# An encoder layer on one core: the gated unit's input split where it is made, reordered on another queue, and its first products in the last attention step

## The chip, the core and the metric

The kernel runs on one core of one Trainium2 chip. A core has a matrix engine (TensorE, PE in the profile, with its weight loads listed as PEld), a vector engine (DVE), a scalar engine (ACT), a general engine (GpSimd, POOL) and a synchronization engine (SyncE, SP). Data reach the on-chip memory SBUF through DMA transfers, which an engine's instruction queue issues; here SP, ACT and POOL all issue some. Each engine takes its instructions in order, so an instruction that waits holds back all that stand behind it on that engine, DMA issues included. Matrix products go into PSUM banks and are read from there by DVE or ACT.

The metric is the time of one execution in microseconds, less being better. The time before is the median of three runs, 1557.84 us (1557.83 to 1558.92).

## The reference

One encoder layer with shared weights is applied to two sequences of 512 tokens with 1024 features, in fp32. Cut to what matters:

```python
h = rms_norm(x, ln1)
q, k, v, u, g_att, g_ssm = split(h @ w_in)
y_att = windowed_attention(rms_norm(q), rms_norm(k), v, sink, bias, mask)   # 16 heads, 4 key/value heads, blocks of 128
y = gelu(s5(u, forward) + s5(u, backward) + d_skip * u)                     # state-space branch, 64 groups of 16 channels
y_ssm = y * sigmoid(y @ w_glu + b_glu)                                      # the gated unit
mixed = sigmoid(g_att) * y_att + sigmoid(g_ssm) * y_ssm
x = x + mixed @ w_out
out = x + square(relu(rms_norm(x, ln2) @ w_up)) @ w_down
```

The change concerns `y`, the output of the state-space branch, and the product `y @ w_glu` that reads it.

## The kernel before

**Products.** An fp32 product is made of three matmuls on rounded operands. An operand is split into a high part, its value rounded to fp32r by a copy on ACT, and a low part, the remainder, by a subtraction on DVE. `mm3` (L148 to L152) issues high times high, high times low, low times high into one PSUM bank. Products of the first half of the kernel share three banks, `acc()`; the `sps` banks are two.

**Stages.** In the trace of before: input norm and tables up to about 230 us; the scan of the state-space branch, a chain of DVE operations, 233 to 343 (L577 to L586); the state outputs, 343 to 430 (L599 to L630); the attention's prelude and steps, 430 to 734; the gated unit (L1030 to L1053), 711 to 833; the output product, the second norm and the MLP to the end. The MLP is a Strassen-like scheme and is not touched.

**State outputs.** The 64 groups are taken two at a time, in 32 rounds `q`. A round makes six matmuls of 128 columns into one `sps` bank (L612, L615), and Gelu (L619) writes the result into `ysb`. After every eight groups one DMA on ACT's queue (L629) stores `ysb` to `y_scr` in DRAM. Loads of the next `u_sb`, `toep` (every eight groups) and `ctab` (every four) stand on POOL's queue, one batch ahead. `pull` puts products of other input blocks between the rounds, and these fill PE.

**Attention.** There are four key/value heads `j` and two sequences `sq`, so eight steps; each has four query blocks `qb`, called units here. The order on PE, ACT and DVE is written out by hand in a manual schedule. Next to a unit's scores and softmax stand matmuls of the previous unit's values (`prev`) and, through `project`, 24 products of the next step's queries (`Tile.project`, L712). The last step has no next step, so its `project` is `nop`. `rows` is the Tile whose queries are turned next; `lower` is a weight split's second half, held until a later place. In a step's second and fourth unit `Divide` handles the previous step: it stores reciprocal row sums to `rs_scr` (L824) and loads them spread over partitions as `fac` (L829), both on SP's queue, and `multiply` (L834) applies them and stores to `mix_scr` (L835). Only the last Divide, after the steps, uses POOL's queue. The weights of the next heads are loaded on SP (L669) and split.

**Reorder of y.** `y_scr` has the chunk position `t` (eight of them) outermost, and the gated unit wants channels on partitions. Eight DMAs from DRAM to DRAM (L900, 512 KB each, on SP) in the units of steps 1 and 2 copy `y_scr[t]` into `y2_scr`.

**Tail and gated unit.** After step 6 the pool `hpool`, with the split input rows `hT`, is closed, and two slots `slot_a` and `slot_b` take its place, which hold the operands `yT`. After the last step the last unit's values are finished, the last Divide runs, and a loop over eight row blocks `m` loads y (L1007) and splits it for each sequence (L1012 on ACT, L1013 on DVE); the read of y has a step, which also puts the tokens into their order. Then the gated unit: for each weight column `m` the column is loaded and split (`c_hi` at L121, `c_lo` at L122), and for each sequence `s` three tiles are loaded on POOL's queue (L1037: attention output, and two gates), the sum of y's two parts gives y again (`yy`, L1043), two multiplications prepare the gates (L1044, L1045), 24 matmuls make the product (`proj_T`), ACT applies the sigmoid (L1048), DVE multiplies and adds (L1049, L1050), and the result is split into `mixT` (L1051, L1052). After each column one row of `w_out` is loaded and split (L1024 to L1026). The second half of `w_out` goes into `slot_a` once the gated unit has read it. `out_half` then makes the output product of each block of 128 tokens and half of `w_out`, 24 matmuls each.

Of the kernel before, what the change touches and what calls it, by code (L numbers as in the profile page):

```python
# [12 lines left out]
F32 = mybir.dt.float32  # L13
# [6 lines left out]
P = 128  # L20
# [20 lines left out]
CH = 16  # L41
# [22 lines left out]
def hybrid_layer(ctx, tc, x, rel, onehot, ln1, w_qkv, w_ug, vectors, lam, coefs, w_glu, w_out, ln2,  # L64
# [15 lines left out]
    def acc():  # L80
        return ps_acc.tile([P, 512], F32, tag="acc", name="acc")
# [8 lines left out]
    y_scr = dram.tile([T, CH, GROUPS, NSEQ * NCHUNK], F32, name="y_scr")  # L90
    y2_scr = dram.tile([GROUPS, CH, T, NSEQ * NCHUNK], F32, name="y2_scr")
# [62 lines left out]
    def proj_T(w, m, act):  # L154

        ps = acc()
        for k in range(KT):
            ws = [t[:, k, m * P:(m + 1) * P] for t in w]
            mm3(ps, ws, [t[:, k, :] for t in act], k == 0, k == KT - 1)
        return ps  # L160
# [5 lines left out]
    hpool_cm = tc.tile_pool(name="hpool", bufs=1, side="right")  # L166
    hpool = hpool_cm.__enter__()
    hT = [[hpool.tile([P, KT, HALF], F32R, name=f"hT{s}_{i}") for i in range(2)] for s in range(NSEQ)]
# [261 lines left out]
    with tc.tile_pool(name="hst", bufs=1) as hp:  # L430
# [127 lines left out]
        with tc.tile_pool(name="ssmo", bufs=2) as sp:  # L558
# [20 lines left out]
            for i in range(1, NCHUNK - 1):  # L579
                t1 = sp.tile([P, 2, GROUPS, NSEQ], F32, tag="t1", name="t1", bufs=1)  # L580
                t2 = sp.tile([P, 2, GROUPS, NSEQ], F32, tag="t2", name="t2", bufs=1)
                V.tensor_mul(t1, h[:, i], a8r)
                V.tensor_mul(t2, h[:, i, ::-1], a8i)
                V.tensor_add(t1, t1, h[:, i + 1])
                V.tensor_add(h[:, i + 1], t1, t2)
                pull(15)  # L586
# [12 lines left out]

            states = [state_rows(0), state_rows(1)]  # L600
            for q in range(GROUPS // SH):
                g0 = q * SH
                if g0 % SB == 0:
                    u_sb, toep = ahead.pop(0)
                    ysb = sp.tile([P, SB, NSEQ * NCHUNK], F32, tag="ysb", name="ysb")
                if g0 % SI == 0:
                    ctab = ahead_c.pop(0)
                st = states.pop(0)
                ps = sps()
                for g in range(SH):  # L610
                    o = ps[:, g * P:(g + 1) * P]
                    PE.matmul(o, toep[:, g0 % SB + g].rearrange("p t c -> p (t c)"), u_sb[:, g0 % SB + g, :],  # L612
                              start=True, stop=False)
                    for ri in range(2):
                        PE.matmul(o, ctab[:, g0 % SI + g, ri, 0:T * CH],  # L615
                                  st[:, ri, g].rearrange("p s k -> p (s k)"), start=False, stop=ri == 1)
                if q + 2 < GROUPS // SH:
                    states.append(state_rows(q + 2))
                S.activation(ysb[:, g0 % SB:g0 % SB + SH, :].rearrange("p g k -> p (g k)"), ps[:, 0:SH * P],  # L619
                             AF.Gelu_apprx_tanh)  # L620

                pull(-(-(phase["units"] - 84) // (GROUPS // SH - q)))
                if (g0 + SH) % SI == 0 and g0 + SH + 2 * SI < GROUPS:
                    ahead_c.append(load_table(g0 + SH + 2 * SI))
                if (g0 + SH) % SB == 0 and g0 + SH + SB < GROUPS:
                    ahead.append(load_batch(g0 + SH + SB))
                if (g0 + SH) % SB == 0:
                    ga = g0 + SH - SB
                    S.dma_start(y_scr[:, :, ga:ga + SB].rearrange("t c g k -> (t c) (g k)"),  # L629
                                ysb.rearrange("p g k -> p (g k)"))  # L630
# [4 lines left out]
    with tc.tile_pool(name="att", bufs=2, reuse_waits="tile") as ap, tc.tile_pool(name="attc", bufs=1, reuse_waits="tile") as ac:  # L635
# [63 lines left out]
        class Tile:  # L699


            def __init__(self, j, sq, t):
                self.key, self.t, self.k, self.qn = (j, sq), t, 0, None
                self.ps = acc()[:, 0:CB]
# [26 lines left out]
            def turn(self):  # L731
                self.pt = acc()
                for h in range(G):
                    PE.transpose(self.pt[0:64, h * P:(h + 1) * P], self.qn[:, h], ident)
# [102 lines left out]

        def whole_block(src, pool, tag, bufs):
# [37 lines left out]
        def nop(*_):  # L876
            pass

        def pieces_of(i):

            if i == 0:
                return weight_pieces(1)
            if i % 2 == 1:
                pending[:] = weight_pieces(i // 2 + 2) if i // 2 + 2 < N_KV else []
                return pending[:2]
            return pending[2:]

        pending = []
        prev = owed = lower = None
        with tc.manual_schedule(engines={mybir.EngineType.PE, mybir.EngineType.Activation, mybir.EngineType.DVE}):  # L890
            for i, (j, sq) in enumerate(steps):
# [4 lines left out]
                for qb in range(NB):  # L896
                    if 1 <= i < 3:

                        t = (i - 1) * NB + qb
                        SP.dma_start(y2_scr[:, :, t, :].rearrange("g c k -> c g k"), y_scr[t])  # L900
# [4 lines left out]
                    project = new.project if new else nop  # L905
                    kd = None
                    if rows and not rows.qn:
                        rows.power()
# [78 lines left out]
                if i == len(steps) - 2:  # L987
                    hpool_cm.__exit__(None, None, None)
                    slot_a = opers.enter_context(tc.tile_pool(name="slot_a", bufs=1, side="right", reuse_waits="tile"))
                    slot_b = opers.enter_context(tc.tile_pool(name="slot_b", bufs=1, side="right", reuse_waits="tile"))  # L990
                    yT = [slot(slot_b), slot(slot_a)]
        owed.add()
        for k in range(prev.nkb):
            prev.turn(k)
            prev.high(k)
            prev.low(k)
            prev.value(k, 0)
            prev.value(k, 1)
        prev.lower_part()
        prev.add()  # L1000
        div = Divide(*steps[-1], *done, True)
        div.invert()
        div.turn()
        div.multiply()
        for m in range(KT):
            yr = (ap if m % 2 else evp).tile([P, T, NSEQ, NCHUNK], F32, tag="c_lo" if m % 2 else "ev", name="yr")
            SP.dma_start(yr.rearrange("p t s k -> p (t s k)"),  # L1007
                         y2_scr[m * 8:(m + 1) * 8].rearrange("g c t k -> (g c) (t k)"))
            for sy in range(NSEQ):
                yv = yr[:, :, sy, :].rearrange("p t k -> p k t")  # L1010
                hi = yT[sy][0][:, m, :].rearrange("p (k t) -> p k t", t=T)
                S.copy(hi, yv)  # L1012
                V.tensor_sub(yT[sy][1][:, m, :].rearrange("p (k t) -> p k t", t=T), yv, hi.bitcast(F32))  # L1013

# [15 lines left out]
    with tc.tile_pool(name="glu", bufs=3, reuse_waits="tile") as gpool:  # L1030
        for m in range(KT):
            w = load_column(w_glu[m], V.tensor_sub)
            for s in range(NSEQ):
# [9 lines left out]
                V.tensor_add(yy, yT[s][0][:, m, :].bitcast(F32), yT[s][1][:, m, :].bitcast(F32))  # L1043
                V.tensor_mul(gs_, gs_, yy)  # L1044
                V.tensor_mul(at, at, ga)  # L1045
                ps = proj_T(w, 0, yT[s])
                gl = gpool.tile([P, HALF], F32, tag="gl", name="gl", bufs=2)
                S.activation(gl, ps, AF.Sigmoid, bias=bglu_sb[:, m:m + 1])  # L1048
# [349 lines left out]
```

## Time and profile before

| | us |
|---|---|
| median of three runs | 1557.84 |
| the profiled execution | 1555.4 |
| its span in the profile | 1553.6 |
| state outputs | about 343 to 430 |
| attention steps 0 to 7, by their row-sum multiplications (L834) of the first and the last | 531.8 to 732.4 |
| products of the gated unit | 711.5 to 826.0 |
| its elementwise work | 741.2 to 833.4 |

The profile is of one execution, so its span is set against that execution's own time: 1.8 us lie around the span. The mean granted clock of TensorE was 0.985 of full speed. DMA moved 237 MB, 165.35 MB read from HBM and 81.82 MB written.

How to read the views: a row of the page's groups names the line, the engine, the operation, its output and inputs with partitions x elements, the count, then busy time and the mean of one instruction in ns, then the idle time of the engine just before and what ended it. A row of the view of stretches gives start and end, length, then busy time with counts for PE, PEld, DVE, ACT and POOL, the granted clock, the DMA share and the rate in GB/s. A row of the timeline gives the start, the duration, engine and line, and in brackets what the instruction waited for. An engine with the letter q (SPq, ACTq) is its queue of DMA issues.

### The profile page before, as it was taken

The numbers are of one execution on the slowest core, as the hardware profiler recorded it, in microseconds if no ns is written. First come the engines' busy times: TensorE is split into PE (matmuls) and PEld (weight loads), VectorE is DVE, ScalarE is ACT, GpSimd is POOL, SyncE is SP. The second block draws the span as 40 slices with busy tenths as digits, with TensorE's granted clock in tenths as the row PEclk, the third lists the DMA queues.
The fourth block names the chain that finished last, engine by engine and source line by source line (L and its number), as shares of the span: only waits on it lengthen the run. The fifth ranks groups of instructions, "written<-read, shape, count | busy, mean of one in ns | idle before, by whom it ended". The sixth has DMA issues, their size and how long they took to land.

```text
span 1553.6 us, 21555 instructions
## 1 busy us (share of the span) xinstructions
PE 1474.7 (95%) x7818; PEld 1246.7 (80%) x7818; DVE 1110.6 (71%) x1997; ACT 768.1 (49%) x1349; POOL 200.6 (13%) x372
## 2 busy tenths in 40 slices
PE   5799999999999899988699989999999999999998
PEld 4688888888999898976577877888888888888787
DVE  8679849994436789887866548777777578666553
ACT  6577761234436687786333325545445434433332
POOL 3033332002331222211320000000000000000000
PEclk9899999999999999999899999999999999999999
DMA  5644448227751413214755214444444595455342
GB/s 181 213 139 164 144 155 297 102 95 272 265 170 40 110 47 84 85 55 141 255 158 166 95 71 160 149 149 150 149 155 150 194 359 198 149 163 163 122 123 67
DMA packets 103531, 237.07 MB, mean 153 GB/s; under 512 B 11994, under 2 KB 31706, under 8 KB 103424
## 3 DMA queue, kind: packets, MB, share of 16 engines
q1 hardware_dynamic: 64784, 134.82, 27.3%
q0 software_dynamic: 16464, 50.39, 9.8%
q10 hardware_dynamic: 22176, 50.47, 8.5%
q8 instruction: 62, 1.02, 0.3%
q14 instruction: 45, 0.37, 0.1%
HBM read 165.35 MB, written 81.82 MB: 159 GB/s over the span
## 4 chain that ended last, share of the span: by engine, by line
PE 53%; issue 17%; DVE 6%; DMA 3%; ACT 3%; POOL 3%; POOLq 0%; SPq 0%; DVEq 0%; ACTq 0%
PE bank L151 13%; PE bank L152 13%; PE bank L150 13%; PE acc L712 3%; PE po L795 2%; PE acc L261 1%; PE sps L763 1%; POOL mx L1037 1%; DVE pl L788 1%; PE tps L779 1%; PE sps L615 1%; DVE p L767 1%; PE acc L150 1%; PE acc L151 1%; PE acc L152 1%
## 5 line engine op out<-in xcount | busy, mean ns | idle before, releaser
L221 PE MATMUL acc<-hT,c_hi 128*128 128x512 f32 x768 | 249.9, 401 | 0.8 <-ACT c_hi L211 0.8
L151 PE MATMUL bank<-b_lo,a_hi 128*128 128x512 f32 x448 | 174.7, 390 | 1.2 <-DVE b_lo L1267 1.2
L152 PE MATMUL bank<-b_hi,a_lo 128*128 128x512 f32 x448 | 174.6, 390 | 0.0
L150 PE MATMUL bank<-b_hi,a_hi 128*128 128x512 f32 x448 | 173.7, 390 | 0.0
L221 PEld LDWEIGHTS acc<-hT,c_hi 128*128 128x128 f32 x768 | 142.5, 190 | 29.9 <-issue 2.2
L221 PE MATMUL acc<-hT,c_lo 128*128 128x512 f32 x384 | 153.3, 400 | 0.5 <-DVE c_lo L212 0.5
L150 PE MATMUL bank<-act,act 128*128 128x512 f32 x376 | 147.3, 392 | 2.2 <-ACT act L1162 2.2
L1266 ACT CAST a_hi<-d_a 128x1024 fp32r<-128x1024 f32 x56 | 58.9, 1052 | 179.1 <-PE bank L151 177.5
L151 PE MATMUL bank<-act,act 128*128 128x512 f32 x376 | 147.1, 391 | 0.0
L152 PE MATMUL bank<-act,act 128*128 128x512 f32 x376 | 146.9, 391 | 0.0
L1267 DVE TENSOR_TENSOR a_lo<-d_a,a_hi 128x1024 fp32r<-128x1024 f32 x56 | 68.5, 1224 | 100.2 <-ACT a_hi L1266 100.2
L712 PE MATMUL acc<-w_hi,hT 128*128 128x256 f32 x512 | 116.1, 295 | 0.0
L151 PEld LDWEIGHTS bank<-b_lo,a_hi 128*128 128x128 f32 x448 | 84.2, 188 | 19.4 <-DVE b_lo L1267 1.9
L152 PEld LDWEIGHTS bank<-b_hi,a_lo 128*128 128x128 f32 x448 | 84.1, 188 | 17.3
L150 PEld LDWEIGHTS bank<-b_hi,a_hi 128*128 128x128 f32 x448 | 84.1, 188 | 17.3
L712 PEld LDWEIGHTS acc<-w_hi,hT 128*128 128x128 f32 x512 | 87.0, 189 | 3.7
L221 PEld LDWEIGHTS acc<-hT,c_lo 128*128 128x128 f32 x384 | 72.9, 190 | 15.2 <-issue 1.0
L773 ACT ACTIVATE p<-p,nmx 128x257 f32<-128x257 f32 (+1 forms) x128 | 72.2, 564 | 25.7 <-DVE nmx L767 24.6
L150 PEld LDWEIGHTS bank<-act,act 128*128 128x128 f32 x376 | 71.0, 189 | 17.4 <-ACT act L1162 2.7
L152 PEld LDWEIGHTS bank<-act,act 128*128 128x128 f32 x376 | 71.0, 189 | 14.9
L151 PEld LDWEIGHTS bank<-act,act 128*128 128x128 f32 x376 | 71.1, 189 | 14.6
L767 DVE CUSTOM_DVE_ANT_0 p<-sps,bias,vec 128x256 f32<-128x256 f32 (+1 forms) x128 | 69.1, 541 | 6.8 <-PE sps L763 5.6
(315 smaller groups left out, 3495.0 us busy)
## 6 DMA issues: line engine op xcount, KB each, us to landing
d_a<-a_scr SPq DMA_DIRECT2D x56, 512.0 KB, 3.6
u_raw<-in_w_up_dram SPq DMA_DIRECT2D x32, 512.0 KB, 5.6
a_scr<-t ACTq DMA_DIRECT2D x64, 256.0 KB, 5.1
k<-in_w_down_dram SPq DMA_DIRECT2D x32, 512.0 KB, 6.0
c_raw<-in_w_ug_dram SPq DMA_DIRECT2D x48, 256.0 KB, 3.3
a_scr<-a ACTq DMA_DIRECT2D x48, 256.0 KB, 2.1
ct_scr<-ctab POOLq DMA_DIRECT2D x16, 576.0 KB, 4.5
ctab_in<-ct_scr POOLq DMA_DIRECT2D x16, 576.0 KB, 7.3
```

Of the source, the lines that this page charges most:

```text
L150: PE.matmul(ps, a[0], b[0], start=first, stop=False)
L151: PE.matmul(ps, a[0], b[1], start=False, stop=False)
L152: PE.matmul(ps, a[1], b[0], start=False, stop=last)
L221: PE.matmul(ps, w[wi][:, k, :], hT[s][hi][:, k, :], start=n == 0, stop=n == 3 * KT - 1)
L261: PE.matmul(ps, hT[t // 4][act][:, k, (t % 4) * P:(t % 4 + 1) * P], wt[:, k % 4, :], start=n == 0, stop=n == 3 * KT - 1)
L615: PE.matmul(o, ctab[:, g0 % SI + g, ri, 0:T * CH], st[:, ri, g].rearrange("p s k -> p (s k)"), start=False, stop=ri == 1)
L712: PE.matmul(self.ps, hT[sq][act][:, k, col:col + P], w[:, k % 4, :], start=i == 0, stop=i == 3 * KT - 1)
L767: V.tensor_tensor_reduce(self.p[:, h, 1:1 + self.nk], self.s[h][:, 0:self.nk], biases[self.j][h][:, b0:b0 + self.nk], -1.0, nsink[:, hh:hh ...
L773: S.activation(p, p, AF.Exp, bias=self.nmx[:, h:h + 1], scale=-1.0, accum_out=self.sums[:, h, self.qb:self.qb + 1])
L795: PE.matmul(self.po, vv, self.hl[i][part], start=i + part == 0, stop=i == self.nkb - 1 and part == 1)
L1266: S.copy(hi, src)
L1267: V.tensor_sub(lo, src, hi.bitcast(F32))
```

## The change

Five things change together.

- **Split at the state outputs.** Gelu writes into a small tile `yg`. ACT copies it, rounded, into a high part, and DVE subtracts one round later to give the low part. Both parts are stored, on ACT's queue, after every four groups: 32 stores of 256 KB in the place of 8 of 512 KB. `y_scr` and `y2_scr` get a leading index for the part. The scan's two temporaries share the tag of the state rows, three buffers in all.
- **Reorder on POOL's queue.** Sixteen DMAs, one in each unit of steps 1 to 4.
- **Loads straight into operands.** `load_y(m)`, two loads of 512 KB each on SP, in the units of steps 6 and 7. `hT` now lies in the two slots themselves, and y takes their place. The rows stay in the order (position, sequence, chunk), so the matmuls of the gated unit read y in runs of 64 elements (`glu_step`), `yy` is written with a step of eight elements, and the sigmoid reads PSUM with a step.
- **Early weight columns.** `glu_pieces` loads and splits the gated unit's columns 0, 1 and 2 in steps 6 and 7.
- **Early products.** In step 7 `project` draws on a generator of the products (0,0) and (0,1), half as many at each place, and (1,0) is drawn in the tail. The tail stands inside the manual schedule, and its value products come after all turns. In step 7 the turned queries' bank is taken ahead of the unit's scores.

The core of the diff:

```diff
@@ state outputs
+            def rounded(y, parts, g):
+                S.copy(parts[0][:, g:g + SH, :], y)
+                return lambda: V.tensor_sub(parts[1][:, g:g + SH, :], y, parts[0][:, g:g + SH, :].bitcast(F32))
+
+            def store_y(parts, ga):
+                for e in range(2):
+                    S.dma_start(y_scr[e, :, :, ga:ga + SI].rearrange("t c g k -> (t c) (g k)"),
+                                parts[e].rearrange("p g k -> p (g k)").bitcast(F32))
...
-            S.activation(ysb[:, g0 % SB:g0 % SB + SH, :].rearrange("p g k -> p (g k)"), ps[:, 0:SH * P],
-                         AF.Gelu_apprx_tanh)
+                if remainder:
+                    remainder()
+                if full:
+                    store_y(*full)
+                    full = None
+                yg = sp.tile([P, SH, NSEQ * NCHUNK], F32, tag="yg", name="yg")
+                S.activation(yg.rearrange("p g k -> p (g k)"), ps[:, 0:SH * P], AF.Gelu_apprx_tanh)
+                remainder = rounded(yg, ysp, g0 % SI)
+                if (g0 + SH) % SI == 0:
+                    full = ysp, g0 + SH - SI
...
-                if (g0 + SH) % SB == 0:
-                    ga = g0 + SH - SB
-                    S.dma_start(y_scr[:, :, ga:ga + SB].rearrange("t c g k -> (t c) (g k)"),
-                                ysb.rearrange("p g k -> p (g k)"))
@@ attention steps
+        def load_y(m):
+            if m % 4 == 0:
+                yT.append([q.rearrange("p (m s) k -> p m (s k)", s=2) for q in slot((slot_b, slot_a)[m // 4])])
+            for e in range(2):
+                SP.dma_start(yT[-1][e][:, m % 4, :].bitcast(F32), y2_scr[e, m * 8:(m + 1) * 8].rearrange("g c t k -> (g c) (t k)"))
+
+        def glu_products(group):
+            for key in group:
+                glu_ps[key] = acc()
+            for k in range(KT):
+                for m, s in group:
+                    yield from glu_step(glu_ps[m, s], glu_w[m], k, s)
+
+        def early_products():
+            yield from glu_products([(0, 0), (0, 1)])
+            yield from glu_products([(1, 0)])
...
+            if i == 6:
+                return glu_pieces(0, ap)
+            if i == 7:
+                return glu_pieces(1, cpool) + glu_pieces(2, cpool)
...
-                    if 1 <= i < 3:
-
-                        t = (i - 1) * NB + qb
-                        SP.dma_start(y2_scr[:, :, t, :].rearrange("g c k -> c g k"), y_scr[t])
+                    if 1 <= i < 5:
+                        e, t = divmod((i - 1) * NB + qb, T)
+                        GP.dma_start(y2_scr[e, :, :, t, :].rearrange("g c k -> c g k"), y_scr[e, t])
+                    for m in {6: (qb,), 7: ((4, 5), (6,), (7,), ())[qb]}.get(i, ()):
+                        load_y(m)
...
-                    project = new.project if new else nop
+                    project = new.project if new else lambda n: glu_pull(n // 2)
...
@@ tail
-        for m in range(KT):
-            yr = (ap if m % 2 else evp).tile([P, T, NSEQ, NCHUNK], F32, tag="c_lo" if m % 2 else "ev", name="yr")
...
-                S.copy(hi, yv)
-                V.tensor_sub(yT[sy][1][:, m, :].rearrange("p (k t) -> p k t", t=T), yv, hi.bitcast(F32))
+            owed.add()
+            glu_pull(6)
+            for k in range(prev.nkb):
+                prev.turn(k)
+                prev.high(k)
+                prev.low(k)
+                glu_pull(4)
...
+            div.invert()
+            glu_pull(24)
+            div.turn()
+            div.multiply()
@@ gated unit
-            w = load_column(w_glu[m], V.tensor_sub)
+            w = glu_w[m] if m in glu_w else load_column(w_glu[m], V.tensor_sub)
...
-                V.tensor_add(yy, yT[s][0][:, m, :].bitcast(F32), yT[s][1][:, m, :].bitcast(F32))
+                parts = [q[:, m % 4].bitcast(F32).rearrange("p (t s k) -> p t s k", t=T, s=NSEQ)[:, :, s, :] for q in yT[m // 4]]
+                V.tensor_add(yy.rearrange("p (k t) -> p t k", t=T), *parts)
...
-                ps = proj_T(w, 0, yT[s])
+                ps = glu_ps.get((m, s))
+                if ps is None:
+                    ps = acc()
+                    for k in range(KT):
+                        for _ in glu_step(ps, w, k, s):
+                            pass
...
-                S.activation(gl, ps, AF.Sigmoid, bias=bglu_sb[:, m:m + 1])
+                S.activation(gl.rearrange("p (k t) -> p k t", t=T), ps.rearrange("p (t k) -> p k t", t=T), AF.Sigmoid, bias=bglu_sb[:, m:m + 1])
```

84 lines of the change are left out of this document (42 added, 42 removed).

## The prediction

> **What bounds the kernel now.** I read the page first, then stretches of time, then the timeline inside the stretch that has room.
>
> ```profile
> span 1553.6 us, 21555 instructions
> PE 1474.7 (95%) x7818; PEld 1246.7 (80%) x7818; DVE 1110.6 (71%) x1997; ACT 768.1 (49%) x1349; POOL 200.6 (13%) x372
> ```
>
> TensorE (PE) is busy 95% of the span. The change removes no matmul, so it can only win PE's idle time, about 79 us in all, or lose more of it. The next view gives the stretches that it touches: columns are start:end, length, busy time of PE, PEld, DVE, ACT and POOL with counts, granted clock, DMA share, GB/s.
>
> ```profile
> 360.90:371.90 11.00, 10.74 (x71) 9.44 (x71) 5.80 (x8) 4.21 (x8) 2.95 (x4) 1.00 0.98 347
> 382.90:394.00 11.10, 9.91 (x69) 8.82 (x68) 5.64 (x8) 4.21 (x9) 2.05 (x4) 1.00 1.02 380
> 404.00:414.00 10.00, 10.00 (x90) 10.00 (x89) 5.62 (x9) 5.43 (x10) 3.86 (x7) 1.00 1.01 351
> ...
> 682.00:711.50 29.50, 22.25 (x101) 15.29 (x99) 27.64 (x61) 26.52 (x58) 2.37 (x5) 0.88 0.29 90
> ...
> 741.00:759.00 18.00, 5.58 (x11) 3.48 (x12) 17.31 (x29) 4.89 (x8) 6.45 (x12) 0.62 0.83 287
> 759.00:826.00 67.00, 64.79 (x278) 52.92 (x277) 49.16 (x79) 24.63 (x41) 14.51 (x27) 0.97 0.53 169
> 826.00:850.00 24.00, 23.06 (x98) 17.96 (x97) 13.38 (x20) 8.78 (x15) 0.00 (x0) 1.00 0.61 194
> ```
>
> At the state outputs (first three rows) PE is full, ACT and DVE have half their time free, and DMA is at its limit in every second stretch. In the last attention step (682 to 711) it is the reverse: DVE and ACT are over 90% busy, PE idles 7.3 us. From 741 to 759 PE idles 12.4 us at a clock of 0.62, and DVE is full. These are the two gaps that the change aims at.
>
> **What it removes: the split of y.**
>
> ```profile
> L1012 ACT CAST act<-yr 128x512 fp32r<-128x512 f32 x16 | 16.9, 1096 | 0.2 <-DMA yr<-y_scr 0.2
> L1013 DVE TENSOR_TENSOR act<-yr,act 128x512 fp32r<-128x512 f32 x16 | 16.9, 1074 | 0.7 <-ACT act L1012 0.4
> ...
> 648.65 1.22 DVE L834 TENSOR_TENSOR ya<-ya,fac 128x1024 f32<-128x1024 f32 x1
> 677.25 1.22 DVE L834 TENSOR_TENSOR ya<-ya,fac 128x1024 f32<-128x1024 f32 x1
> 709.48 1.21 DVE L834 TENSOR_TENSOR ya<-ya,fac 128x1024 f32<-128x1024 f32 x1
> ```
>
> 17 us on each of ACT and DVE go from the attention's end. L834 stands once in every step's fourth unit: one step takes 28.6 us (648.65 to 677.25), the one beside the splits 32.2. The new last step has, per unit, 12 products of 512 columns for 24 of 256, about the same PE time; I take 28.6 and win 3.6 us. From L834 to the last Divide's store (709.48 to 733.96, below) I keep the 24.5 us of before: the tail loses its splits and gains 24 products.
>
> ```profile
> 733.96 0.75 POOL L835 DMA_DIRECT2D mix_scr<-ya  x1 [6.94 <-DVE ya L834]
> 734.74 0.58 POOL L1037 DMA_DIRECT2D mx<-mix_scr  x1
> 741.21 0.69 DVE L1045 TENSOR_TENSOR mx<-mx,mx 128x512 f32<-128x512 f32 x1 [2.44 <-DMA mx<-ga_scr]
> ```
>
> This chain stays: the gates' loads (mx) stand on POOL's queue behind the last Divide. So the elementwise work of the gated unit, which began at 741.2, begins near 737.6.
>
> **The first products** (72 of 384) move ahead of it. They fill PE, but take no time off the end by themselves: they occupy all three acc banks, two gl buffers let two more products through, and then PE waits for the elementwise work again. What ends the stage is that work.
>
> ```profile
> 755.86 0.79 PE L152 MATMUL acc<-act,c_lo 128*128 128x512 f32 x1 [5.45 <-DVE c_lo L122]
> ...
> 764.17 0.68 DVE L1049 TENSOR_TENSOR gl<-gl,mx 128x512 f32<-128x512 f32 x1
> ...
> 771.17 0.68 DVE L1049 TENSOR_TENSOR gl<-gl,mx 128x512 f32<-128x512 f32 x1
> 772.15 0.54 POOL L1037 DMA_DIRECT2D mx<-gs_scr  x1
> 776.02 0.69 DVE L1044 TENSOR_TENSOR mx<-mx,yy 128x512 f32<-128x512 f32 x1 [0.97 <-DMA mx<-gs_scr]
> ...
> 825.17 0.68 DVE L1049 TENSOR_TENSOR gl<-gl,mx 128x512 f32<-128x512 f32 x1
> ...
> 832.69 0.69 DVE L1052 TENSOR_TENSOR act<-gl,act 128x512 fp32r<-128x512 f32 x1 [0.69 <-ACT act L1051]
> 833.30 0.69 DVE L1026 TENSOR_TENSOR act<-w_raw,act 128x512 fp32r<-128x512 f32 x1
> ```
>
> Its 16 units (a column m and a sequence s each) end at 833.4, 92 us after 741.2. From the fifth unit to the fourteenth (L1049 at 764.17 and at 825.17, nine steps) each takes 6.8 us: L1049 frees a gate buffer, POOL reloads it, L1044 of a unit further on waits for the load and stands in DVE's order before the next L1049. PE needs 0.235 us a product (98 in 23.06, above), 24 of them 5.6 us, so this loop, not PE, sets the pace, and PE's lead of three banks fills up.
>
> Now DVE's own need. Back-to-back operations of 0.69 us start 0.61 apart (832.69, 833.30). A unit has six: 3.7 us. The sum yy (L1043) now writes with a step of eight elements; no row has such a write on DVE. Bounds are 0 and the +0.39 of L1013's stepped read (1.07 against 0.69); I take 0.39. The sigmoid gl now reads PSUM with steps: L234, which does so, takes as long as L236, which does not (586 ns both), so 0.
>
> ```profile
> L234 ACT COPY up<-acc x16: 576/586/607, 35.0 to 175.6; 128x512 f32<-128x512 f32 x16
> L236 ACT COPY sg<-acc x6: 583/586/587, 343.1 to 403.9; 128x512 f32<-128x512 f32 x6
> ```
>
> Five weight columns stay to be split here (10 x 0.6) and eight rows of w_out (8 x 0.6): 10.8 us, 0.7 a unit. So 4.8 us a unit at DVE's full rate, 6.8 by the loop. Before, four products lay ready at 741; now five do, and the wait for c_lo (5.45) of column 2 is gone, since columns 0 to 2 are split in steps 6 and 7 (six casts and six subtractions of 0.6 on engines that lost 17 us each). With products ready DVE ran 17.31 of 18 us, so I am nearer to the full rate: 5.5 us a unit, 88 us, end at 825.6. The output products of both sequences need it: the 48th lies near 826.5, and their second weight half, loaded only after the last product, is by then ready. 50 more at 0.235 bring the 98th to about 838, where before stood 850: **-12 us**. At 4.8 us the end is 815 and the same sum -22; the second weight half would then come late and take some of it back, so I bound it at -18. By the loop from the fifth unit on it is 5 x 4.8 + 9 x 6.8 + 8 (the last two, 825.2 to 833.4) = 93 us, 831, and -6.
>
> The matmuls read y in runs of 64 elements instead of 512. No row has this; bounds 0 and, if it cost a tenth, 384 x 0.023 = 9 us on a PE that waits; I take 0. [...]
>
> **The reorder on POOL.** Eight transfers leave SP's queue, sixteen come to POOL's.
>
> ```profile
> 517.10 0.34 SPq L824 DMA_DIRECT2D rs_scr<-row  x1
> 517.54 6.26 SPq L669 DMA_DIRECT2D w_raw<-in_w_qkv_dram  x2
> 523.86 0.52 SPq L900 DMA_DIRECT2D y_scr<-y_scr  x1
> 524.47 1.28 SPq L829 DMA_DIRECT2D fac<-rs_scr  x2
> 531.76 1.23 DVE L834 TENSOR_TENSOR ya<-ya,fac 128x1024 f32<-128x1024 f32 x1 [4.38 <-DMA fac<-rs_scr]
> ...
> 556.18 1.26 SPq L829 DMA_DIRECT2D fac<-rs_scr  x2
> 558.02 0.34 SPq L669 DMA_DIRECT2D w_raw<-in_w_qkv_dram  x1
> ```
>
> In step 1 fac is issued 7.4 us after rs, behind two weight loads and a reorder; DVE stands 4.4 us and PE with it. In step 2, without reorders, fac goes ahead of the weight and nothing waits. Step 1 now resembles step 2: between 0 and -4.4, I take **-3**. [...] On POOL an issue of this kind costs 0.76 us (L556); POOL is busy 13% of the span, and the row powers behind it leave gaps of 31.2/9 = 3.5 us on average. But sixteen may be drawn forward to the last key products near 440, where the power is on the path, and fac now shares SP in steps 6 and 7 with sixteen y loads: 0 to +9 (twice the 4.4), I take **+1**.
>
> ```profile
> L556 POOL DMA_DIRECT2D toep_scr<-lag_scr x8: 763/764/780, 233.7 to 240.1; - x8
> POOL ms L724 <- DVE ms L722: 31.2, 9, 4.7
> ```
>
> **What it adds at the state outputs.** 32 casts and 32 subtractions of 256 elements, near L619's 0.38 and L274's 0.43: 12 and 14 us over 85 us, on engines half free beside a full PE, so nothing; without that cover, 12 to 14. ACT's queue gains 24 issues of 0.33 us; each pair waits for a DVE subtraction, and the next Gelu stands behind it, with one sps bank to spare.
>
> ```profile
> L619 ACT ACTIVATE ysb<-sps 128x256 f32<-128x256 f32 x32 | 12.3, 384 | 42.1 <-PE sps L615 42.1
> L274 DVE TENSOR_TENSOR keys<-acc,rk 128x256 f32<-128x256 f32 x4 | 1.7, 425 | 6.5 <-POOL rk L273 6.5
> L629 ACTq DMA_DIRECT2D y_scr<-ysb x8: 326/326/327, 355.7 to 429.3; - x8
> DMA to landing us min/median/max: 6.0/8.8/12.7
> ```
>
> The stores cost DMA: 4 MB more. Before, 380 GB/s was the most, so 0.52 MB per batch of eight groups is 1.4 us more in stretches of 10.9 us, three of which are full. The last row is the landing of toep: the slowest already exceeds the 10.9 us for which a load runs ahead, and PE lost 1.5 us there. 0 to 3 x 1.5 = +4.6; I take **+3**, as the full stretches have no slack.
>
> **Sum**: -12 - 3 + 1 + 3 = -11 us. Against the profiled execution (1555.4 us: span 1553.6 and 1.8 around it) that is 1544.4; the median of the runs is 2.4 higher, so 1546.8.
>
> **Rivals.**
> - DVE at its full rate (4.8 us a unit), no loss at the state outputs, all of step 1: -18 - 4.4 = -22, 1535. For it: 17.31 of 18. Against: waits for loads in every later unit. 20%.
> - The loop keeps 6.8 us, since its order is that of before: -6 + 4.6 + 1 = 0, 1557 to 1558. The first products would then be work that was hidden anyway. For it: nine units in a row at that pace. 12%.
> - Slower: the loads of the state outputs. If each of six batches lands 3 us late, +18 in the place of +3: +4, 1562. It decides from a toep landing near 14 us on average (now 8.8); ACT held by its stores would add. Against: the even stretches have room. 12%.
> - The change does not do what it says: the first products wait in the last step for y (their loads follow the release of hT at the end of step 6) and hold PE's whole queue: from a load's issue to its first use the gates took 6.5 us (734.74 to 741.21), so +6.5, 1553. 6%.
>
> **Chances.** The forecast, within 1538 to 1554, 50%. The range 1532 to 1560 takes in the first, second and last rivals. A measurement of this kernel tells about 0.2% (3.1 us) from no change: faster 0.77, same 0.11, slower 0.12.
>
> **What would show it.** Right: no split of y beside the last attention step and its length near 28.6 us; the first L1045-like product near 738; L1049's spacing near 5.5; no 4.4 us wait in step 1. Wrong: PE idle beyond 5 us at the state outputs with toep as releaser; a wait for y rows inside the last step; a spacing of 6.8.

## The result and the profile after

The changed kernel takes 1569.14 us (median of four runs, 1564.72 to 1571.20) where the kernel before takes 1557.84 (1556.14 to 1558.92 over four). The ratio is 1.0072, 95% interval 1.0055 to 1.0089: **slower by 0.7%, some 11 us, where 11 us faster was forecast**, and outside the range given. The profiled execution took 1564.72 us; its span is 9.3 us longer than before.

The head of the page after:

```profile
span 1562.9 us, 21674 instructions
PE 1474.4 (94%) x7818; PEld 1249.3 (80%) x7818; DVE 1113.0 (71%) x2013; ACT 765.8 (49%) x1365; POOL 211.7 (14%) x388
```

Over the whole span PE has the same busy time and the same number of matmuls as before, so the 9.3 us are PE's idle time. To find the place, one takes marks that both kernels have and subtracts. The first mark, the third of step 0's scores on PE, is a fair one: 2748 matmuls stand ahead of it in both traces.

| mark, us from the span's start | before | after | difference |
|---|---|---|---|
| third score of step 0 | 479.31 | 501.10 | +21.8 |
| row-sum multiplication of step 0 | 531.76 | 550.88 | +19.1 |
| the same of step 5 | 677.25 | 695.92 | +18.7 |
| the same of step 6 | 709.48 | 722.72 | +13.2 |
| the same of step 7 (last Divide) | 732.44 | 744.33 | +11.9 |
| end of the span | 1553.6 | 1562.9 | +9.3 |

So everything is lost **ahead of step 0's third score**, in the last key products and the attention's prelude, and from there to the end the changed kernel wins 12.5 us. The view of stretches shows the loss; first before, then after (columns as in the prediction).

```profile
440.00:450.00 10.00, 8.44 (x70) 8.03 (x69) 7.13 (x14) 3.90 (x8) 3.95 (x8) 1.00 0.54 170
450.00:460.00 10.00, 10.00 (x88) 10.00 (x86) 2.75 (x6) 2.50 (x5) 2.53 (x4) 1.00 0.51 144
460.00:470.00 10.00, 10.00 (x87) 10.00 (x86) 3.29 (x7) 2.12 (x5) 1.83 (x3) 1.00 0.01 2
```

```profile
440.00:450.00 10.00, 4.78 (x26) 4.54 (x26) 5.88 (x11) 4.94 (x10) 0.41 (x2) 0.82 0.81 312
450.00:460.00 10.00, 7.26 (x46) 7.30 (x47) 2.54 (x6) 0.38 (x1) 6.12 (x10) 0.67 0.65 211
460.00:470.00 10.00, 4.50 (x33) 3.97 (x32) 2.12 (x5) 0.76 (x2) 4.50 (x6) 0.84 0.24 84
470.00:480.00 10.00, 10.00 (x72) 10.00 (x72) 2.33 (x4) 2.12 (x4) 1.53 (x4) 0.81 0.22 73
```

Before, PE runs almost without a gap. After, it is idle for nearly half of 440 to 470, no other engine is busy for more than 61% of any of these stretches, and the granted clock falls to 0.67. Engines that all wait for one another point to an order, not to a load. PE's waits from 436 to 512 after (total, times, longest):

```profile
PE acc L747 <- DVE qn L742: 7.5, 3, 4.6
PE acc L725 <- DVE keys L272: 4.8, 1, 4.8
PE acc L259 <- DVE keys L272: 4.8, 1, 4.8
PE acc L725 <- DVE va L664: 0.9, 1, 0.9
```

PE waits for the norms of keys and queries. Each needs a sum on DVE, a power on POOL and a product on DVE before PE gets its bank or its operand. POOL adds a small constant to the sum (L270 for a key, L737 for a query) and then takes the power (L271, L738). The timeline of POOL after shows what stands between the two:

```profile
443.52 0.22 POOL L270 TENSOR_SCALAR ms<-ms 128x4 f32<-128x4 f32 x1 [4.57 <-DVE ms L268]
448.12 0.19 POOL L768 COPY p<-vec 128x4 f32<-128x4 f32 x1 [4.38 <-DVE w_lo L897]
450.02 0.19 POOL L768 COPY p<-vec 128x4 f32<-128x4 f32 x1 [1.71 <-DVE w_lo L897]
450.25 0.80 POOL L951 DMA_DIRECT2D y_scr<-y_scr  x1
451.08 1.05 POOL L271 TENSOR_TENSOR rk<-ms,neg_half 128x4 f32<-128x4 f32 x1
...
456.04 0.22 POOL L270 TENSOR_SCALAR ms<-ms 128x4 f32<-128x4 f32 x1
458.52 0.22 POOL L737 TENSOR_SCALAR ms<-ms 128x4 f32<-128x4 f32 x1 [2.26 <-DVE ms L735]
465.42 0.22 POOL L737 TENSOR_SCALAR ms<-ms 128x4 f32<-128x4 f32 x1 [6.68 <-DVE ms L735]
465.70 0.78 POOL L951 DMA_DIRECT2D y_scr<-y_scr  x1
466.51 1.05 POOL L271 TENSOR_TENSOR rk<-ms,neg_half 128x4 f32<-128x4 f32 x1
467.53 1.00 POOL L738 TENSOR_TENSOR rq<-ms,neg_half 128x4 f32<-128x4 f32 x1
```

The key's power (L271) that belongs to the sum at 443.52 starts at 451.08: two copies of sinks into score tiles of step 0 (L768) stand ahead of it and wait for the split of the weights, whose buffers they take over, and then a reorder of y (L951). The power of the sum at 456.04 stands behind the sum of a query tile that arrives at 465.42, and so does the power of the query tile whose sum came at 458.52: it starts at 467.53, and PE's longest wait for qn, 4.6 us, ends behind it at 469.05. Reorders meant for steps 1 to 4 are issued here, two among the last keys and twelve by 489. DVE's order has changed as well; after:

```profile
440.17 2.58 DVE L897 TENSOR_TENSOR w_lo<-w_in,w_hi 128x512 fp32r<-128x512 f32 x4 [5.38 <-ACT w_hi L896]
442.67 0.42 DVE L272 TENSOR_TENSOR keys<-acc,rk 128x256 f32<-128x256 f32 x1
```

The keys' product (L272) stands behind four weight splits that wait for their load and cast. Its power was ready by 438.0 (L271 at 436.96). In the prelude no engine's order is written by hand, and POOL's is not in the steps either; it is laid down when the program is built. Sixteen more issues on POOL gave another order.

A wait cost more than its length here, as two rows of PE after, ahead of and behind the first wait, show (pairs of the same matmul):

```profile
436.81 0.40 PE L259 MATMUL acc<-c_hi,act 128*128 128x256 f32 x2
...
444.38 0.63 PE L259 MATMUL acc<-c_hi,act 128*128 128x256 f32 x2
```

Starts lie 0.21 us apart for 0.12, and the granted clock is 0.50 there (443.2 to 446.4, and likewise 452.8 to 456.5 and 469.8 to 473.5, behind the other two long waits). So the 24 key products behind the first wait take 4.4 us (443.15 to 447.54) and the 24 query products behind the second 4.7 (452.74 to 457.40), where 24 x 0.12 is 2.9. The four rows of waits hold 18.0 us, 16.6 of them ahead of the third score, where the kernel before has 1.6; and the same 2748 matmuls keep PE busy for 455.1 us up to there, where it was 448.6. The 15.0 us of waits and the 6.5 us of slower matmuls make 21.5 of the 21.8. A shorter wait had slower matmuls behind it too: one of 2.3 us that ended at 738.96 was followed, one us on, by starts 0.43 us apart for 0.23 up to 743.4, at a granted clock of 0.50. The prediction priced no wait that way.

The second half, after: the multiplications of steps 5 to 7, the first product of attention output and gate, three of the gated unit's products (L1100, before L1049).

```profile
695.92 1.22 DVE L847 TENSOR_TENSOR ya<-ya,fac 128x1024 f32<-128x1024 f32 x1
722.72 1.22 DVE L847 TENSOR_TENSOR ya<-ya,fac 128x1024 f32<-128x1024 f32 x1
744.33 1.23 DVE L847 TENSOR_TENSOR ya<-ya,fac 128x1024 f32<-128x1024 f32 x1 [8.27 <-DMA fac<-rs_scr]
753.32 0.69 DVE L1091 TENSOR_TENSOR mx<-mx,mx 128x512 f32<-128x512 f32 x1 [2.62 <-DMA mx<-ga_scr]
775.40 0.69 DVE L1100 TENSOR_TENSOR gl<-gl,mx 128x512 f32<-128x512 f32 x1
787.32 0.70 DVE L1100 TENSOR_TENSOR gl<-gl,mx 128x512 f32<-128x512 f32 x1
836.24 0.69 DVE L1100 TENSOR_TENSOR gl<-gl,mx 128x512 f32<-128x512 f32 x1
```

```profile
760.42 0.80 PE L157 MATMUL acc<-act,gc_hi 128*128 128x512 f32 x1 [8.65 <-ACT gl L1099]
777.95 0.80 PE L157 MATMUL acc<-act,c_lo 128*128 128x512 f32 x1 [8.79 <-DVE c_lo L122]
```

The last step is 26.8 us long where it was 32.2, and the tail 21.6 where it was 23.0. The gated unit starts with PE waiting 8.65 us for a bank and, after six units, 8.79 for the split of the fourth column; its elementwise work, 753.3 to the sixteenth L1100 at 841.8, takes 88.4 us where it took 89.4.

### The profile page after: what moved, and what is told of

Read it like the earlier page. It is cut to its first block, busy times and chain, and to the rows that moved or that the text cites. A ratio compares the mean times of both kernels' runs of the same rounds, so it can differ in the third digit from the quotient of the medians.

```text
span 1562.9 us, 21674 instructions
## 1 busy us (share of the span) xinstructions
PE 1474.4 (94%) x7818; PEld 1249.3 (80%) x7818; DVE 1113.0 (71%) x2013; ACT 765.8 (49%) x1365; POOL 211.7 (14%) x388
## 3 DMA queue, kind: packets, MB, share of 16 engines
q8 instruction: 62, 1.02, 0.3%
## 4 chain that ended last, share of the span: by engine, by line
PE 52%; issue 17%; DVE 9%; DMA 4%; POOL 2%; ACT 2%; ACTq 0%; SPq 0%; POOLq 0%; DVEq 0%
PE bank L151 13%; PE bank L152 13%; PE bank L150 13%; PE acc L725 3%; PE po L808 1%; DVE pl L801 1%; PE sps L776 1%; DVE p L780 1%; PE acc L150 1%; PE acc L152 1%; PE acc L151 1%; DMA w_raw<-in_w_out_dram 1%; PE tps L792 1%; DMA mx<-mix_scr 1%; DVE ya L818 1%
## 5 line engine op out<-in xcount | busy, mean ns | idle before, releaser
L219 PE MATMUL acc<-act,c_hi 128*128 128x512 f32 x768 | 249.9, 401 | 0.9 <-ACT c_hi L209 0.9
L219 PEld LDWEIGHTS acc<-act,c_hi 128*128 128x128 f32 x768 | 142.7, 190 | 30.0 <-issue 2.2
L219 PE MATMUL acc<-act,c_lo 128*128 128x512 f32 x384 | 153.4, 400 | 0.5 <-DVE c_lo L210 0.5
L725 PE MATMUL acc<-w_hi,act 128*128 128x256 f32 x512 | 117.7, 298 | 5.7 <-DVE keys L272 4.8
L725 PEld LDWEIGHTS acc<-w_hi,act 128*128 128x128 f32 x512 | 88.2, 192 | 9.8 <-issue 5.0
L219 PEld LDWEIGHTS acc<-act,c_lo 128*128 128x128 f32 x384 | 72.8, 190 | 15.4 <-issue 1.0
L780 DVE CUSTOM_DVE_ANT_0 p<-sps,bias,vec 128x256 f32<-128x256 f32 (+1 forms) x128 | 69.1, 541 | 10.3 <-PE sps L776 8.9
```

The lines of the kernel that those rows point to most:

```text
L219: PE.matmul(ps, w[wi][:, k, :], hT[s][hi][:, k, :], start=n == 0, stop=n == 3 * KT - 1)
L725: PE.matmul(self.ps, hT[sq][act][:, k, col:col + P], w[:, k % 4, :], start=i == 0, stop=i == 3 * KT - 1)
L780: V.tensor_tensor_reduce(self.p[:, h, 1:1 + self.nk], self.s[h][:, 0:self.nk], biases[self.j][h][:, b0:b0 + self.nk], -1.0, nsink[:, hh:hh ...
```

## The experiments

Each kernel ran beside the kernel before on the same chip; ratios are to that, with their 95% intervals, and set runs from different chips side by side. The marks are from each run's profile.

| run | median us | ratio, interval | first multiplication (step 0) | span |
|---|---|---|---|---|
| before | 1557.84 | 1 | 531.8 | 1553.6 |
| changed | 1569.14 | 1.0072, 1.0055 to 1.0089 | 550.9 | 1562.9 |
| r1 | 1542.74 | 0.9911, 0.9895 to 0.9928 | 526.4 | 1540.4 |
| r2 | 1557.55 | 1.0001, 0.9991 to 1.0010 | 542.4 | 1557.8 |
| r3 | 1543.06 | 0.9903, 0.9886 to 0.9921 | 526.6 | 1541.4 |
| r4 | 1541.11 | 0.9893, 0.9879 to 0.9908 | 526.6 | 1540.2 |
| r5 | 1557.12 | 1.0001, 0.9989 to 1.0012 | 541.2 | 1553.8 |
| r6 | 1541.70 | 0.9894, 0.9877 to 0.9911 | 528.3 | 1540.2 |
| r7 | 1538.52 | 0.9875, 0.9861 to 0.9890 | 526.2 | 1537.1 |
| r8 | 1535.75 | 0.9859, 0.9844 to 0.9875 | 528.1 | 1533.2 |
| r9 | 1546.26 | 0.9932, 0.9913 to 0.9952 | 531.8 | 1545.0 |
| r10 | 1553.88 | 0.9985, 0.9971 to 1.0000 | 538.4 | 1552.5 |
| r11 | 1539.07 | 0.9891, 0.9874 to 0.9908 | 527.2 | 1536.1 |
| r12 | 1562.59 | 1.0028, 1.0018 to 1.0038 | 546.4 | 1557.9 |

### Where the reorders are issued: r1, r2, r3

**r1**, POOL in the written order in the steps:

```diff
-        with tc.manual_schedule(engines={mybir.EngineType.PE, mybir.EngineType.Activation, mybir.EngineType.DVE}):
+        with tc.manual_schedule(engines={mybir.EngineType.PE, mybir.EngineType.Activation, mybir.EngineType.DVE, mybir.EngineType.Pool}):
```

> Only change to the changed kernel: in the attention steps POOL, too, keeps the order in which the program is written, so no reorder of y can go out ahead of its unit in steps 1 to 4. Theory (reorders and the sinks' copies drawn forward on POOL's queue stand ahead of the powers of the key and query norms, and the prelude loses some 21 us): the second score of step 0 moves from 501.1 to about 480, the waits of PE for keys and qn between 438 and 512 (4.8, 4.8, 4.6, 1.5 us) go, and the time falls by about 20 us to 1547-1551. Rival (the prelude loses because the weights' load starts 2.9 us later behind the state outputs, and their splits stand ahead of the keys): the waits stay, time within 3 us of 1569. Rival (the sixteen transfers themselves, wherever they stand, take DMA bandwidth from the loads): the loss moves into steps 1 to 4 and the time falls by less than 8 us.

All three signs came, and more time than expected: 25 us below the changed kernel (ratios 1.0072 and 0.9911), the third score (the mark that the expectation calls the second) at 478.4, and 14 us below the kernel before. The same sixteen transfers cost nothing that shows where they stand in steps 1 to 4. DVE's order in r1:

```profile
438.66 0.42 DVE L272 TENSOR_TENSOR keys<-acc,rk 128x256 f32<-128x256 f32 x1 [1.48 <-POOL rk L271]
439.00 2.49 DVE L897 TENSOR_TENSOR w_lo<-w_in,w_hi 128x512 fp32r<-128x512 f32 x4
```

The keys go first, and the four splits follow. The late weights fall as a cause: their load goes out at 433.6 in the changed kernel and at 431.6 in r1, which is 2.0 us against a gain of 25; and in r9 and r10 (below) it goes out at 432.7 and 433.1, and only r10 has the waits for keys.

**r2** and **r3**, the reorders on another queue:

```diff
-                        GP.dma_start(y2_scr[e, :, :, t, :].rearrange("g c k -> c g k"), y_scr[e, t])
+                        SP.dma_start(y2_scr[e, :, :, t, :].rearrange("g c k -> c g k"), y_scr[e, t])   # r2
+                        S.dma_start(y2_scr[e, :, :, t, :].rearrange("g c k -> c g k"), y_scr[e, t])    # r3
```

> Only change to the changed kernel: the sixteen reorders of y on SP's queue in place of POOL's, in the same units. Theory (POOL's order is what cost the prelude): the waits for keys and qn in the prelude go, as in r1, and the time falls to about 1550; the wait of DVE for fac in step 1 (4.4 us before the change) may come back, so 1548-1555. Rival (late weights): within 3 us of 1569. Rival (bandwidth): a fall of less than 8 us.

> Only change to the changed kernel: the sixteen reorders on ACT's queue, which keeps the written order. Theory: prelude as before the change, sixteen issues of 0.33 us on ACT in steps 1 to 4 cost at most 5 us, neither SP nor POOL delayed: 1546-1553. Rival (late weights): within 3 us of 1569. Rival (bandwidth): a fall of less than 8 us.

r3 is as good as r1 and below its expected time; ACT's order is written by hand, so its issues stand in their steps. r2 gains 11 us of the 25 and lies above its expected 1548 to 1555: SP's order is not written by hand, and it has changed here. One reorder went ahead of the prelude's loads, and the load of the second sequence's keys (L903), which in r1 goes out at 444.1, behind the weights, stands ahead of them. SP's queue in r2:

```profile
433.56 0.61 SPq L951 DMA_DIRECT2D y_scr<-y_scr  x1
434.46 9.77 SPq L903 DMA_DIRECT2D kn<-keys  x2
444.34 2.37 SPq L894 DMA_DIRECT2D w_in<-in_w_qkv_dram  x4
```

The second key load waits for the last keys, so the weights (L894) go out at 444.3, not at 433.6 as in the changed kernel. PE's waits in r2, 436 to 545, show that and the stall of step 1, which is back:

```profile
PE acc L725 <- ACT w_hi L896: 5.3, 1, 5.3
PE po L808 <- DVE ya L818: 5.2, 1, 5.2
PE tps L707 <- POOL kd L698: 2.9, 1, 2.9
```

Three queues, the same transfers: POOL and ACT in written order give 0.991 and 0.990, SP gives 1.000, and POOL without a fixed order 1.007. What differs is the order on the issuing queue, and what stands behind the issue there.

### What of the order costs: r5, r9, r10, r12

**r5** has ten of the reorders early, but POOL's order otherwise written; **r9** and **r10** are its two halves.

```diff
+        with tc.manual_schedule(engines={mybir.EngineType.Pool}):
+            reorder(1)                 # r5, r10
+            kd = key_copies(0, 0)
+            reorder(1)                 # r5, r10
...
+                new.power()
+                reorder(2)             # r5, r9
```

> r1 with ten of the sixteen reorders as early as in the changed kernel (two with the last keys, eight among the query norms of the prelude), but each norm's power right behind its sum on POOL, and the rest of POOL in the written order. If the reorders' issues (0.8 us each on POOL) and their traffic (5 MB) cost the prelude: the waits for keys and qn come back and the time is 1557-1569. If the shuffled order did it (a power behind sinks' copies that wait for the split of the weights, behind another tile's sum): PE waits at most 3 us more than in r1 before step 0, and the time is 1541-1547.

> r5 without its first two reorders: eight of the sixteen go out behind the powers of the first four query tiles, eight in steps 1 and 2; DVE keeps its order of r1 up to the last keys. If the eight issues and their 4 MB beside the prelude cost what r5 lost (14 us over r1): 1553-1558. If r5 lost it where two reorders stand among the last keys' powers and DVE takes four splits of the weights ahead of the keys: PE's waits for keys (4.6 and 3.2 us) are gone, at most 4 us are left for qn, 1543-1548.

> The complement of r9: two reorders among the last keys' powers, where r5 and the changed kernel have them, the other fourteen in steps 1 to 4. DVE's order has four and then four more splits of the weights ahead of the keys, as in r5 and the changed kernel. If that order is the cause: PE waits 4 to 5 us and 3 to 5 us for keys, and the time is 8 to 12 us above r1, 1550-1555. If the eight later ones did it: 1542-1546.

r5 lies in the first reading's range: 14 us above r1 (0.0090). But its halves separate. Eight reorders among the query norms, issues and 4 MB together, cost 3.3 us (0.0021, which is within what the two intervals leave open), with three new waits of at most 1.5:

```profile
PE acc L747 <- DVE qn L742: 3.9, 3, 1.5
```

Two among the keys cost 11.5 us (0.0074), and DVE's order in r10 has the four splits ahead of the keys again. DVE and PE's waits in r10:

```profile
439.51 2.64 DVE L897 TENSOR_TENSOR w_lo<-w_in,w_hi 128x512 fp32r<-128x512 f32 x4 [5.23 <-ACT w_hi L896]
442.07 0.42 DVE L272 TENSOR_TENSOR keys<-acc,rk 128x256 f32<-128x256 f32 x1
...
PE acc L259 <- DVE keys L272: 4.6, 1, 4.6
PE acc L725 <- DVE keys L272: 3.2, 1, 3.2
```

So these 11.5 us are neither the issue time (two of 0.8 us) nor the traffic. The two reorders there with DVE's order of r1 were not tried, so that part rests on the waits: both are for keys, behind the splits.

**r12** takes the sinks' copies off POOL in the changed kernel:

```diff
-                GP.tensor_copy(self.p[:, :, 0], nsink[:, j * G:(j + 1) * G])
+                S.copy(self.p[:, :, 0], nsink[:, j * G:(j + 1) * G])
```

> The changed kernel with the sinks' copies into the score tiles made on ACT in place of POOL; the reorders stay where the changed kernel has them on POOL, and so does the order of sums and powers around them. It tells what holds the powers beyond the two early reorders (the changed kernel lies some 11 us above r5). If it is the sinks' copies, which stand on POOL ahead of a key's power and wait for the weights' split until 450: PE's second wait for keys falls from 4.8 to about 3 us and the time by 2 to 6 us, to 1563-1567. If it is the order of sums and powers itself (a key's power behind the sum of a query tile that is 7 us away, at 465): the wait of 4.6 us for qn stays, the time within 2 us of the changed kernel's.

It lies 0.0044 (6.9 us) below the changed kernel, a little more than the 2 to 6 us of the first reading; by the spans it is 5.0. PE's second wait for keys is 3.1, as the first reading had it, and the wait of 4.6 for qn stays, as the second had it:

```profile
PE acc L747 <- DVE qn L742: 6.1, 2, 4.6
PE acc L259 <- DVE keys L272: 4.4, 1, 4.4
PE acc L725 <- DVE keys L272: 3.1, 1, 3.1
```

The 25 us between the changed kernel and r1 thus part into about 11.5 for DVE's order around the keys, 3.3 for eight reorders among the queries, 5 to 7 for the sinks' copies, and some 3 to 5 that are left for sums and powers drawn apart. The split takes it that the parts add up. They are differences between separate runs, and by the intervals of the ratios each is open by 3 to 4 us, so only the first and the third stand clear of noise.

### What the early products are worth: r4, r11

**r4** is r1, and **r11** is r8 (below), without them; the three weight columns are still split early:

```diff
         def glu_pull(n):
-            for _ in itertools.islice(early, n):
-                pass
+            return
```

> r1 without the early products: the weight columns 0 to 2 are still split in steps 6 and 7, but all 384 products of the gated unit are made in their stage. By the prediction's reason (the first products take no time off the end, the elementwise work ends the stage): within 3 us of r1. By the other reading (PE was busy 64.79 of 67 us in that stage, so PE bounds it, and what is done ahead of it is won): 5 to 14 us slower than r1, bounded by 72 products of 0.235 = 17 us less the 8 us that PE waits in the changed kernel once its three banks are full.

> r8 without the early products. If the elementwise work bounds the start of the gated unit also with the gates loaded early: within 2 us of r8 (1534-1537). If PE has become the bound there: 3 to 8 us slower than r8.

Without them r1 is not slower (0.9893 against 0.9911): the last step and the tail get 2.6 us shorter, and PE then waits for the same elementwise work (10.3 us for the sigmoid's output, 11.5 in r1). r11 is 0.0032 (5 us) slower than r8, though the intervals touch. In its trace the loads of fac are issued 5.7 us behind the row sums' store, for 2.0 in r8, and the last multiplication comes 0.7 us later, behind a last step that is 1.1 us shorter. Why, and where the rest of the 5 us goes, stays open, so r11 does not show that PE became the bound.

### What waits in the gated unit: r6, r7, r8

**r6** loads a column ahead of the row of `w_out`, **r7** moves the last Divide's transfers to ACT's queue, **r8** does both:

```diff
+            if 2 <= m < KT - 1:                                                    # r6, r8
+                glu_w[m + 1] = load_column(w_glu[m + 1], V.tensor_sub)
             row_piece(w_rows[0], 0, m, cpool.tile([P, HALF], F32, tag="c_raw", name="w_raw"))
...
-                self.queue = GP if last else SP
+                self.queue = S if last else SP                                     # r7, r8
```

> r1 with each weight column from the fourth on loaded ahead of the row of w_out that stands before it, so that its two halves no longer wait for a c_raw buffer which that row's late split holds. Theory (the 8 us wait for c_lo at the fourth column is this buffer): the wait goes, L1049's successor shows no 12 us gap between its sixth and seventh unit, and the time is 5 to 8 us below r1: 1535-1538. Rival (DVE's elementwise loop sets the end whatever the column does): within 2 us of r1.

> r1 with the last Divide's three transfers on ACT's queue in place of POOL's, so that the first gate loads do not stand behind its store. Theory (the elementwise work begins only when POOL has stored the last Divide and then loaded its first tiles, 5.2 us behind the multiplication's issue): the first product of attention output and gate comes 3 to 7 us earlier against the multiplication, PE's wait of 8.5 us for a bank shrinks by as much, and the time is 3 to 6 us below r1: 1537-1540. Rival (the buffer memory of the gate tiles comes free only with the Divide, or ACT stands still behind its transfers): within 2 us of r1.

> r6 and r7 together: if both waits are on the path and do not hide one another, their gains add up, 8 to 14 us below r1: 1529-1535. If the end is set by DVE's own work in the gated unit (six operations of 0.6 to 1.1 us, 4.0 us a unit, plus splits), the second gain is smaller than alone.

r6 is a miss: within the interval of r1. The wait for the fourth column is still 6.9 us, and the gap of 11.9 us between the sixth and seventh unit stays: ACT casts the column at 737.7, but DVE's part of the split comes at 753.4, in DVE's order behind six units of elementwise work at 4.0 us each, so an earlier load does not help. r7 gains 0.0036 (5.6 us). DVE in r7:

```profile
720.47 1.23 DVE L847 TENSOR_TENSOR ya<-ya,fac 128x1024 f32<-128x1024 f32 x1 [8.04 <-DMA fac<-rs_scr]
...
725.92 0.68 DVE L1091 TENSOR_TENSOR mx<-mx,mx 128x512 f32<-128x512 f32 x1
```

The elementwise work begins 5.5 us behind the multiplication, not 9.0, since POOL loads the first gates before the last Divide. PE's wait for a bank does not shrink (11.2 us), it moves. r8 has the lowest median, 1535.75 us, 1.4% below the kernel before. By the ratios it is 8.1 us below r1 (7.0 by the medians), at the lower end of the 8 to 14 expected; but its 2.5 us below r7 are within the intervals, as r6's 2.6 below r1 were, so a gain of the earlier column is not shown.

## Why the prediction was wrong

- **The step that failed: "sixteen may be drawn forward to the last key products near 440, where the power is on the path".** The mechanism was named and the place was right, but it was a term of +1 with an upper bound of +9, "twice the 4.4" of a stall on SP. It measured about 25 us (changed against r1), 22.7 of them before step 0's third score. The bound counted issue time and one stall, and no rival had it larger. What it left out is that the issues change the order of everything on a queue whose order isn't fixed, and of DVE through it, and that each of the waits of 4.6 to 4.8 us was followed by 3.2 to 3.7 us at a granted clock of 0.50. The trace of before already had such a move: of the eight reorders on SP, written for the units of steps 1 and 2, four went out from 445.5 on, right behind a key load and ahead of step 0.
- **The same transfers from another queue: no difference** where both orders are the written one: r1 (POOL) and r3 (ACT) are alike (0.9911 and 0.9903). The time went into the instructions behind the issue.
- **State outputs, +3: too dear.** From the first matmul on `st` to the last took 85.9 us for 83.9, and 83.9 in r1. PE's waits from 343 to 432 after are

```profile
PE sps L622 <- ACT st L592: 1.4, 1, 1.4
PE sps L619 <- DMA toep<-toep_scr: 1.2, 2, 0.8
PE sps L619 <- ACT yg L632: 1.1, 2, 0.6
```

  against 1.4 for toep before (the prediction took 1.5, and 4.6 for three times as much; it is 4.2). The loads' waits did not grow although the stores did; 1.1 us are new, where Gelu stands behind a store that waits for DVE. The rival of late loads, which was to make the kernel slower, did not come: it wanted a landing of toep near 14 us, and the median is 9.0 for 8.8.
- **Step 1, -3: right.** From the third score to step 0's multiplication 49.8 us for 52.5 (-2.7), and in r1 48.0. DVE's wait for fac, 4.4 us before, is gone there.
- **The last step and the gated unit, -12: right sign, -9.4** (from step 5's multiplication to the end, 867.0 us for 876.4), though not where it was put. The last step won 5.4, where 3.6 were taken, and the tail 1.4, where none were; the rest is the gated unit and what follows, 2.6, where 8.4 were taken. The loop's pace was to be 5.5 us a unit throughout. It was 4.0 for six units, with the gates in and DVE busy 21.74 of the 22.08 us from 753.32 to 775.40, then a gap of 11.9, then 7.0 (787.32 to 836.24, seven units), as in the rival that kept 6.8. Before, it was 3.8 for four units, then a gap of 9.7, then 6.8: the change gave the fast stretch two more units and left the rest nearly as it was. (ACT, said to be over 90% busy in the last step before, was 89.9%, which changes nothing.)
- **The first products, worth nothing: right** (r4). PE took them and then waited 8.65 us.
- **The stepped write of yy, +0.39: +0.46.** L1089 takes 1.14 us, where L1043 took 0.69. The sigmoid's stepped read of PSUM took 0.68 us both times, as forecast, and the matmuls that read y in runs of 64 elements took 405 ns in the mean (c_hi), where they took 403 to 409: nothing, as forecast, where the 0 was the author's choice between two bounds.
- **y's loads did not wait**: no wait of PE for y in steps 6 and 7, and PE is busy 26.67 of the 26.80 us from step 5's multiplication to step 6's.

Without the failed term the sum was -12, 1545.8 on the scale of the medians; r1, the change with POOL in order, has 0.9911 times 1557.84 = 1544.0. That they lie so close is partly luck: by the spans r1 wins 8.1 us from step 5's multiplication on, where 12 were forecast, and makes it up with 4.4 in step 1 for 3 and 0.9 won ahead of it for 3 lost.

## What to carry to other kernels

Moving a transfer's issue to another engine's queue is a change of that engine's order: list what stands behind it, and if the order isn't fixed by the program, expect the builder to draw the issue forward, far from where it was written, and to lay the instructions around it in another order. A bound for such a term has to hold the whole path through that queue, not the issue's length, and a long wait of PE is to be priced with the slower matmuls behind it (here 24 of them took 4.4 and 4.7 us for 2.9; waits of 2.3 and of 3.2 to 4.8 us had them, the wait of 1.5 us that ended at 485.6 had not). Early work for an engine that later waits for another one was no gain here (r1 has 0.9911 with it, r4 0.9893 without).

## What the hardware showed that had not been expected

Long waits of PE cost a third as much again: 24 matmuls of 256 columns took 4.4 and 4.7 us behind waits of 4.8, for 2.9 without one. A wait of 3.2 us did it as well, in r10 at 450.6: starts 0.21 us apart for 5.9 us behind it, for 0.12. Stores of 8 MB in place of 4 MB in the state outputs, where DMA was already at its limit in three stretches (0.98 to 1.02), cost the loads beside them nothing that PE felt: 1.2 us of waits for 1.4.
